# A two-layer diffusion trunk: all elementwise work of GpSimd on VectorE, and new durations in the scheduler

## The chip, the cores and the metric

The kernel runs on one core of a Trainium2 chip. The metric is the device time of one launch in microseconds, median of several runs. TensorE (PE), VectorE (DVE), ScalarE (ACT), GpSimd (POOL) and SyncE (SP) each carry out their own list of instructions in order and meet through semaphores. Here SP and POOL also issue DMAs.

## What is computed

Two layers over 256 latent and 256 context tokens with 1024 channels. A layer is a half-step SwiGLU FFN (2816 wide), a token mixer, and a second half-step FFN; each lies between a norm ahead of it (`sublayer_in`, with shift and scale from the conditioning vectors) and one behind it (`sublayer_out`, gated, onto the residual).

```python
def rmsnorm(x, g):
    xf = x.astype(jnp.float32)
    y = xf * lax.rsqrt(jnp.mean(xf * xf, axis=-1, keepdims=True) + EPS)
    return (y * g.astype(jnp.float32)).astype(x.dtype)

def sublayer_in(h, g_pre, mod, s):
    return rmsnorm(h, g_pre) * (1 + mod[:, 3 * s + 1]) + mod[:, 3 * s]

def sublayer_out(h, y, g_post, mod, s, weight):
    return h + weight * mod[:, 3 * s + 2] * rmsnorm(y, g_post)

def swiglu(h, w_gate, w_up, w_down):
    return (jax.nn.silu(h @ w_gate) * (h @ w_up)) @ w_down
...
    for l in range(DEPTH):
        last = l == DEPTH - 1
        mod_x = (silu_c @ ada_w[l] + ada_b[l]).reshape(B, N_ADA, 1, D_MODEL)
        mod_c = (silu_cc @ ada_w[l] + ada_b[l]).reshape(1, N_ADA, 1, D_MODEL)
        y = swiglu(sublayer_in(x, norm_pre[l, 0], mod_x, 0), ffn_w_gate[l, 0], ffn_w_up[l, 0], ffn_w_down[l, 0])
        x = sublayer_out(x, y, norm_post[l, 0], mod_x, 0, FFN_RESIDUAL_WEIGHT)
        ...
        y_x, y_c = token_mixer(
            sublayer_in(x, norm_pre[l, 1], mod_x, 1), sublayer_in(ctx, norm_pre[l, 1], mod_c, 1),
            cos, sin, not last, w_in[l], ...)
        x = sublayer_out(x, y_x, norm_post[l, 1], mod_x, 1, 1.0)
        y = swiglu(sublayer_in(x, norm_pre[l, 2], mod_x, 2), ffn_w_gate[l, 1], ffn_w_up[l, 1], ffn_w_down[l, 1])
        x = sublayer_out(x, y, norm_post[l, 2], mod_x, 2, FFN_RESIDUAL_WEIGHT)
        ...
    return x
```

The mixer (left out) projects its input once and runs two branches on it: latent attention with eight heads and a rotary part, and a bidirectional diagonal state-space layer (S5, 64 groups of 64 states) with a gated output. Both are projected, gated, merged and projected again. Context tokens read only context; layer 1 gives out the latent tokens alone, so its mixer's end and its second FFN work on 256 columns instead of 512.

## The kernel before

Activations stand with channels on partitions and tokens on the free axis: eight blocks of 128 channels by 512 columns, in two halves `h` = 0 and 1 of 256 columns each. Matmuls reach float32 accuracy by splitting both sides in a high and a low part: each weight block of 128x512 is loaded (`raw`), rounded by ScalarE (`whi`), and its remainder formed by VectorE (`wlo`); then three matmuls are added up (high by high, low by high, high by low). Activations are split likewise (`hhi`, `hlo` for a norm's output, `hi`, `lo` elsewhere).

The program is recorded first. `Recorder` takes every operation with the operations it depends on, `schedule` (L379) simulates the five engines with durations from `cost` (L275), latencies from `LATENCY` and prices for a switch of ScalarE's table (`TABLE`) and of TensorE's tile width (`TILE`), and picks at each moment the ready operation with the smallest key. A key is the amount of TensorE work of the main line recorded ahead of the operation; work recorded aside has a shift. What comes out is one fixed list per engine, which `emit` (L572) writes, so that every row of the trace says L576. A duration in `cost` thus never changes how long an operation takes, only the order. Building layer 1's state-space tables (`s5_build`, L1598) is a filler: during layer 0's second FFN it is shifted by `PACE_B` times the VectorE time it has used so far. Layer 0's build is paced likewise by `PACE_A`. `ada_rows` forms the conditioning rows on VectorE as another filler (`ar`, `aj`, `crow` and the accumulator `ah`).

Where one sublayer ends and the next begins, three functions work. `close` (L765) evacuates a block `y` of the output and forms for each half three tiles `tri` whose column sums are needed: the residual with itself, the output with itself, and the product of both, `xy`; TensorE sums them into the bank `misc`. `Norm.chain` (L2043) makes from these sums the inverse root of the norm behind the sublayer and, through `ve`, that of the norm ahead of the next one. Each is `rsqrt` (L719), a dozen steps on 128x64 tiles `rs` on VectorE: an integer step on the bits first, two iterations, and a 128x256 tile `sp`, which TensorE spreads over all partitions (`spread`, L755) into the banks `b1` and `b2`. `Norm.block` (L2072) then forms for each block `po` = y times b1, the new residual x + po (written over `x`, or as a new tile `xn` in layer 1's last transition, where `xonly` is set), `pn` = x times b2, and its two parts `hhi` on ScalarE and `hlo` on VectorE, with which the next matmuls begin. The transition has all this in a row for each half.

GpSimd has a share in this. In `close`, the products `xy` of 54 blocks run there; in `block`, the residual sums of 48 half-blocks and the eight `xn`. In layer 1's last transition GpSimd also multiplies the identity's columns into the first `sp` (`mask`), and the first two blocks' `po` (`EARLY` = 2), for which ScalarE copies b1 out of its bank. In the trace a product `xy` is `tri<-x,y` and a residual sum `x<-x,po` or `xn<-x,po`. GpSimd's queue also carries 322 DMA issues (staging of the state-space tables `stg`, `ur`, `ys`, `kd`, and others) and sixteen memsets `X`.

In the mixer, attention takes heads in pairs. For each, scores go into a bank, VectorE forms the maximum `mx`, ScalarE the exponential `pr` with it, and VectorE the reciprocal `ss`; `qr` is the rotary query, `qs` its share of the next scores, `rot` the rotation, `rp` the product with the sine. Between them `s5_run` (L1740) puts the S5 work of the same layer: complex products `t` with the tables `m1l`, two scans `w` over 512 columns each (TENSOR_TENSOR_SCAN), and the rotated states `X`.

## Time and profile before

| | us |
|---|---|
| runs | 2303.83, 2302.32, 2298.68 |
| median | 2302.32 |
| the profiled execution, its own time | 2301.47 |
| its span, first to last instruction | 2299.7 |
| TensorE busy | 2236.4 |
| VectorE busy | 1870.4 |
| ScalarE busy | 1034.4 |
| GpSimd busy | 297.0 |

The span is what the trace covers; 1.8 us of the profiled execution's time lie around it. Busy time counts every stretch in which at least one operation of an engine runs, and a matmul's end is modelled. "Idle before" in a row of groups is time in which the engine did nothing right before operations of that group, and the names behind `<-` are what ended it. The granted clock is TensorE's, as a share of 2.4 GHz; 0.5 is its lower level of 1.2 GHz, and a figure between is a mean over a stretch.

### The profile page before, as it was taken

What the parts mean: (1) busy time and instruction counts of PE and PEld (TensorE: products, weight loads), DVE (VectorE), ACT (ScalarE), POOL (GpSimd) and SP (SyncE); (2) the same over time, 40 slices, a digit from 0 to 9 for tenths busy, and PEclk for the clock granted to TensorE, in tenths of its full rate; (3) what the DMA queues carried; (4) which work ended last, traced back from release to release, by engine and by line L of the source; (5) the groups of instructions that cost most, each with busy time, mean ns of one, the idle gap of its engine ahead of it and who ended that gap; (6) DMA issues with size and microseconds to landing.
All of it is one profiled execution on the core that took longest, in us unless ns stands there. A gap on an engine that the chain in (4) does not pass through costs nothing.

```text
span 2299.7 us, 43776 instructions
## 1 busy us (share of the span) xinstructions
PE 2236.4 (97%) x15768; PEld 1926.3 (84%) x15768; DVE 1870.4 (81%) x4314; ACT 1034.4 (45%) x2050; POOL 297.0 (13%) x455
## 2 busy tenths in 40 slices
PE   8999999899999999999999989999999998998998
PEld 6888778787888888888888878888888897997997
DVE  4997878979989889699997999888557579886454
ACT  5332233653347644543222453333246446675452
POOL 0010011330100300200100231110003110312000
PEclk9999999999999999999999989999999999998999
DMA  9344556954975556133554644566444695773552
GB/s 312 102 163 137 172 203 205 359 199 154 319 260 172 170 163 217 48 128 117 176 183 139 210 148 158 200 213 220 152 147 150 236 319 179 186 258 111 179 193 87
DMA packets 237481, 428.06 MB, mean 186 GB/s; under 512 B 29488, under 2 KB 58032, under 8 KB 237264
## 3 DMA queue, kind: packets, MB, share of 16 engines
q1 hardware_dynamic: 213904, 350.79, 47.2%
q0 software_dynamic: 23360, 74.48, 9.2%
q8 instruction: 124, 2.03, 0.4%
q14 instruction: 93, 0.76, 0.1%
HBM read 366.56 MB, written 58.59 MB: 185 GB/s over the span
## 4 chain that ended last, share of the span: by engine, by line
PE 75%; DVE 8%; DMA 3%; issue 1%; ACT 1%; POOL 0%; DVEq 0%; SPq 0%; ACTq 0%; POOLq 0%
PE acc L576 74%; DVE rs L576 1%; DVE t L576 1%; DVE wlo L576 1%; DMA aw<-in_ada_w_dram 1%; PE misc L576 1%; DVE lo L576 1%; DVE w L576 1%; DMA ar<-in_ada_t_dram 0%; DMA m1l<-stg 0%; DMA raw<-in_w_in_dram 0%; DVE po L576 0%; DVE hlo L576 0%; DVE X L576 0%; DVE sp L576 0%
## 5 line engine op out<-in xcount | busy, mean ns | idle before, releaser
L576 PE MATMUL acc<-hhi,whi 128*128 128x256 f32 (+2 forms) x2112 | 717.8, 345 | 5.1 <-ACT hhi L576 4.2
L576 PE MATMUL acc<-hlo,whi 128*128 128x256 f32 (+2 forms) x2112 | 703.9, 344 | 4.8 <-DVE hlo L576 4.8
L576 PE MATMUL acc<-hhi,wlo 128*128 128x256 f32 (+2 forms) x2112 | 706.3, 343 | 0.5 <-DVE wlo L576 0.2
L576 ACT ACTIVATE whi<-raw 128x512 fp32r<-128x512 f32 x802 | 479.0, 624 | 366.7 <-PE acc L576 141.3
L576 DVE TENSOR_TENSOR wlo<-raw,whi 128x512 fp32r<-128x512 f32 x802 | 530.1, 689 | 133.1 <-ACT whi L576 80.3
L576 PEld LDWEIGHTS acc<-hhi,whi 128*128 128x128 f32 (+1 forms) x2112 | 398.7, 190 | 57.2 <-ACT hhi L576 7.0
L576 PEld LDWEIGHTS acc<-hhi,wlo 128*128 128x128 f32 (+1 forms) x2112 | 399.0, 190 | 49.4 <-DVE wlo L576 2.8
L576 PEld LDWEIGHTS acc<-hlo,whi 128*128 128x128 f32 (+1 forms) x2112 | 392.3, 190 | 55.2 <-DVE hlo L576 7.7
L576 PE MATMUL acc<-hi,whi 128*128 128x512 f32 (+1 forms) x1144 | 390.7, 344 | 2.4 <-DVE lo L576 2.0
L576 PE MATMUL acc<-lo,whi 128*128 128x512 f32 (+1 forms) x1144 | 388.6, 341 | 0.0
L576 PE MATMUL acc<-hi,wlo 128*128 128x512 f32 (+1 forms) x1144 | 384.2, 343 | 1.0 <-DVE wlo L576 1.0
L576 PEld LDWEIGHTS acc<-hi,whi 128*128 128x128 f32 x1144 | 215.3, 189 | 32.3 <-DVE lo L576 2.4
L576 PEld LDWEIGHTS acc<-hi,wlo 128*128 128x128 f32 x1144 | 214.4, 189 | 27.8 <-DVE wlo L576 2.2
L576 PEld LDWEIGHTS acc<-lo,whi 128*128 128x128 f32 x1144 | 215.5, 189 | 25.0 <-issue 0.9
L576 ACT ACTIVATE sg<-acc 128x512 f32<-128x512 f32 (+1 forms) x129 | 64.9, 504 | 231.5 <-PE acc L576 212.9
L576 ACT ACTIVATE hi<-sg 128x512 fp32r<-128x512 f32 (+1 forms) x113 | 60.6, 542 | 167.9 <-DVE sg L576 142.2
L576 DVE TENSOR_TENSOR sg<-sg,acc 128x512 f32<-128x512 f32 (+1 forms) x97 | 55.7, 575 | 97.0 <-ACT sg L576 62.0
L576 POOL TENSOR_TENSOR tri<-x,y 128x256 f32<-128x256 f32 x54 | 52.4, 976 | 320.5 <-ACT y L576 299.0
L576 POOL DMA_DIRECT2D stg<-P x64 | 34.8, 543 | 376.7 <-DVE P L576 360.9
L576 DVE CUSTOM_DVE_ANT_0 ar<-ar,crow,adab 128x512 f32<-128x512 f32 x104 | 79.0, 760 | 3.6 <-DMA ar<-in_ada_t_dram 3.4
L576 DVE CUSTOM_DVE_ANT_0 ar<-ar,crow,ah 128x512 f32<-128x512 f32 x104 | 79.0, 759 | 2.0 <-DMA ar<-in_ada_t_dram 1.1
L576 DVE TENSOR_TENSOR lo<-sg,hi 128x512 fp32r<-128x512 f32 (+1 forms) x113 | 65.6, 586 | 16.9 <-ACT hi L576 10.8
(249 smaller groups left out, 3234.5 us busy)
## 6 DMA issues: line engine op xcount, KB each, us to landing
raw<-in_w_gu_dram SPq DMA_DIRECT2D x352, 256.0 KB, 3.2
ar<-in_ada_t_dram SPq DMA_DIRECT2D x208, 256.0 KB, 3.5
raw<-in_w_dn_dram SPq DMA_DIRECT2D x176, 256.0 KB, 3.1
raw<-in_w_sq_dram SPq DMA_DIRECT2D x128, 256.0 KB, 4.3
raw<-in_w_in_dram SPq DMA_DIRECT2D x112, 256.0 KB, 5.2
m1l<-stg SPq DMA_DIRECT2D x96, 256.0 KB, 5.1
aw<-in_ada_w_dram SPq DMA_DIRECT2D x80, 256.0 KB, 5.8
stg<-P POOLq DMA_DIRECT2D x64, 256.0 KB, 3.4
```

What stands on the lines that cost most here:

```text
L576: getattr(getattr(self.tc.nc, engine), method)(*[real(v) for v in a], **{k: real(v) for k, v in kw.items()})
```

## The change

`xy` in `close`, the first `sp` in layer 1's last transition, its first two `po`, and all residual sums go to VectorE; ScalarE's copy of b1 goes away with them. GpSimd keeps the DMA issues and the memsets. `PACE_B` becomes 3.2 instead of 2.5. In the scheduler, a GpSimd DMA issue is taken at 545 ns instead of 1038, its data 400 ns later; a switch of TensorE's tile width at 180 instead of 90; a scan of 512 columns at 1134 ns instead of 600; a one-pass matmul of 512 columns at 226.8 instead of 215.8 and of 256 columns at 120 instead of 109; TensorE's operations with fewer than 128 columns of weights cheaper.

```diff
@@ -22,7 +22,7 @@
 FF_SEGS = (6, 6, 5, 5)
 LEAD = 6
 LATE_A, LATE_B, LATE_C, URGENT = 0, 15000, 10000, 1500
-PACE_A, PACE_B = 1.6, 2.5
+PACE_A, PACE_B = 1.6, 3.2
 WINDOW, SOON, TABLE_PULL, TILE_PULL = 15000, 0, 8000, 12000
 SLOTS, HALVES, ROWS, TRIS = 70, 8, 8, 4
 W_AHEAD = 10000
@@ -37,7 +37,7 @@
 STAT_PULL = 1000
 LAG = 0
 SLOW = 1.0
-RUSH, APART, HOLD, EARLY = False, True, 0.8, 2
+RUSH, APART, HOLD = False, True, 0.8
 FB, LAST = 22, 4
 FIRST = (5000, 1000, 1000, 1000)
 BEHIND = 1000
@@ -228,7 +228,7 @@
     LATENCY = {("PE", "PE"): 0, ("PE", "DVE"): 196, ("PE", "ACT"): 197, ("PE", "POOL"): 224, ("PE", "SP"): 190,
                ("DVE", "DVE"): 127, ("DVE", "PE"): 202, ("ACT", "ACT"): 153, ("ACT", "PE"): 230}
     SPARE = {"slot": 8}
-    TABLE, TILE = 1283, 90
+    TABLE, TILE = 1283, 180
     TABLES = {AF.Silu: 1, AF.Sigmoid: 2, AF.Exp: 3, AF.Gelu_apprx_tanh: 4}
 
     def __init__(self, tc):
@@ -277,14 +277,14 @@
         out = a[0]
         n = int(np.prod(out.shape[1:])) if isinstance(out, View) else 0
         if method == "dma_start":
-            return 1038 if eng == "POOL" else 525
+            return 545 if eng == "POOL" else 525
         if eng == "PE":
             lhs, rhs = (a[1], a[2]) if method == "matmul" else (a[1], a[2])
             passes = 1 if rhs.dt != F32 else 4 if method == "matmul" else 2
             m = max(lhs.shape[-1], 32)
-            if m < 128:
-                return 28 + max(n, m) * passes * m / 307.2
-            return 2.5 + max(n * passes / 2.4, 53.3 * min(passes, 2) * (1 if method == "transpose" else 2))
+            if m < 128 and passes > 1:
+                return 6 + n * passes * m / 307.2
+            return (13.5 if passes == 1 else 4) + n * passes / 2.4
         if eng == "ACT":
             ptr = sum(isinstance(kw.get(k), View) for k in ("bias", "scale"))
             return 155 + 0.714 * n + 60 * ptr + 70 * ("accum_out" in kw)
@@ -296,6 +296,8 @@
             return 67 + 1.04 * int(np.prod(a[1].shape[1:]))
         if method == "tensor_tensor_reduce":
             return 132 + 1.042 * n
+        if method == "tensor_tensor_scan":
+            return 67 + 2.083 * n
         if method == "reciprocal":
             return 70 + 6.2 * n
         return 67 + 1.042 * n + (62 if method == "scalar_tensor_tensor" and isinstance(a[2], View) else 0)
@@ -502,7 +504,7 @@
                 op.start = t
                 free[e] = op.end = t + op.dur + extra
                 if op.bytes:
-                    dma = max(dma, op.end + self.DMA_IN + 1000 * (e == "POOL")) + op.bytes / 360.0
+                    dma = max(dma, op.end + self.DMA_IN + 1400 * (e == "POOL")) + op.bytes / 360.0
                     op.end = dma
                 if op.main:
                     self.front = max(self.front, op.key)
@@ -716,11 +718,10 @@
             out = self.region(r, n)[32 * j:32 * j + 32].rearrange("p (r k) -> p r k", r=n)
             self.nc.tensor.matmul(out, self.ones, q[:, :, j], start=False, stop=False, skip_group_check=True)
 
-    def rsqrt(self, v, plain=False, wide=True, times=1.0, mask=None):
+    def rsqrt(self, v, plain=False, wide=True, times=1.0):
 
         nc = self.nc
         end = 1.875 * times
-        mask = mask or nc.vector
         n = v.shape[-1]
         y, w, z = (self.blk(n, name="rs") for _ in range(3))
         nc.vector.tensor_scalar(y.bitcast(I32), v.bitcast(I32), -0.5, 1595932665.0, op0=ALU.mult, op1=ALU.add)
@@ -733,7 +734,7 @@
         diagonal = self.ident[:, 0:128:32].unsqueeze(2).to_broadcast([128, 4, 64])
         for c in range(0, n if wide else 0, 64):
             r = self.blk(256, name="sp").rearrange("p (j k) -> p j k", j=4)
-            mask.tensor_tensor(r, y[:, c:c + 64].unsqueeze(1).to_broadcast([128, 4, 64]), diagonal, op=ALU.mult)
+            nc.vector.tensor_tensor(r, y[:, c:c + 64].unsqueeze(1).to_broadcast([128, 4, 64]), diagonal, op=ALU.mult)
             rows.append(r)
         nc.vector.tensor_scalar(z, w, 0.375 * times, -1.25 * times, op0=ALU.mult, op1=ALU.add)
         nc.vector.tensor_tensor(z, z, w, op=ALU.mult)
@@ -779,7 +780,7 @@
         else:
             nc.scalar.activation(y, src, AF.Copy, scale=G)
             nc.scalar.activation(q2, y, AF.Square)
-            nc.gpsimd.tensor_tensor(xy, x, y, op=ALU.mult)
+            nc.vector.tensor_tensor(xy, x, y, op=ALU.mult)
         self.rec.urgent = False
         self.rec.pull = None if i < NB - 1 else STAT_PULL
         self.stat(3 * h, t, 3)
@@ -2043,7 +2044,6 @@
     def chain(self, h):
         T, v = self.T, self.T.nc.vector
         T.rec.urgent = self.xonly or RUSH
-        mask = T.nc.gpsimd if self.xonly else None
         b1, b2 = self.banks()
         self.bc[h] = T.flat(b1), T.flat(b2)
         if self.post is not None:
@@ -2054,11 +2054,8 @@
                 st = T.blk(128, name="rs")
                 v.tensor_copy(st, T.region(3 * h + 1, 2))
                 v.memset(T.region(3 * h, 3), 0.0)
-            r, rows = T.rsqrt(w, True, times=D ** 0.5, mask=mask)
+            r, rows = T.rsqrt(w, True, times=D ** 0.5)
             T.spread(b1, rows[0])
-            if self.xonly:
-                self.b1 = T.flat(T.blk(256, name="b1"))
-                T.nc.scalar.activation(self.b1, T.flat(b1), AF.Copy)
             a = T.blk(64, name="rs")
             v.tensor_tensor(a, r, st[:, 0:64], op=ALU.mult)
             v.scalar_tensor_tensor(a, st[:, 64:128], 2.0, a, op0=ALU.mult, op1=ALU.add)
@@ -2075,14 +2072,12 @@
         xv = T.part(T.x[i][:], h)
         c = i * 2 + h
         if self.post is not None:
-            t, xo, e = T.flat(T.blk(256, name="po")), xv, nc.vector
+            t, xo = T.flat(T.blk(256, name="po")), xv
             if self.xonly:
                 T.x[i] = T.blk(256, name="xn")
                 xv = T.flat(T.x[i])
-                if i < EARLY:
-                    b1, e = self.b1, nc.gpsimd
-            e.tensor_tensor(t, T.part(self.y[i], h), b1, op=ALU.mult)
-            (nc.vector if i < 2 and not self.xonly else nc.gpsimd).tensor_tensor(xv, xo, t, op=ALU.add)
+            nc.vector.tensor_tensor(t, T.part(self.y[i], h), b1, op=ALU.mult)
+            nc.vector.tensor_tensor(xv, xo, t, op=ALU.add)
         A, B = T.coef[self.pre]
         if self.h[i] is None:
             n = 256 if self.xonly else 512
```

The order of all engines changes with this. VectorE has 113 operations more. Three places of its list follow; the numbers behind names tell tiles apart.

First, VectorE at layer 1's last transition, from the second `sp` on: `y` is the mixer's output, `acc` the bank with a spread root. Before:

```order
L576 TENSOR_TENSOR sp_25539<-rs_25528,ident_83 128x256
L576 TENSOR_TENSOR rs_25532<-rs_25532,rs_25526 128x64
L576 TENSOR_SCALAR rs_25544<-rs_25532 128x64
L576 TENSOR_TENSOR rs_25544<-rs_25544,rs_25532 128x64
L576 SCALAR_TENSOR_TENSOR sp_25539<-rs_25544,sp_25539 128x256
L576 TENSOR_TENSOR po_25550<-y_25234,acc_25519 128x256
L576 TENSOR_TENSOR po_25554<-y_25279,acc_25519 128x256
L576 TENSOR_TENSOR po_25558<-y_25346,acc_25519 128x256
L576 TENSOR_TENSOR pn_25560<-xn_25542,acc_25552 128x256
```

Now:

```order
L578 TENSOR_TENSOR sp_25515<-rs_25508,ident_83 128x256
L578 TENSOR_TENSOR rs_25510<-rs_25510,rs_25506 128x64
L578 TENSOR_SCALAR rs_25518<-rs_25510 128x64
L578 TENSOR_TENSOR rs_25518<-rs_25518,rs_25510 128x64
L578 SCALAR_TENSOR_TENSOR sp_25515<-rs_25518,sp_25515 128x256
L578 TENSOR_TENSOR po_25522<-y_25150,acc_25501 128x256
L578 TENSOR_TENSOR po_25526<-y_25188,acc_25501 128x256
L578 TENSOR_TENSOR xn_25528<-x_85,po_25522 128x256
L578 TENSOR_TENSOR xn_25530<-x_86,po_25526 128x256
L578 TENSOR_TENSOR pn_25532<-xn_25528,acc_25524 128x256
L578 TENSOR_TENSOR pn_25534<-xn_25530,acc_25524 128x256
```

The first two `po` and all `xn`, which were GpSimd's, stand between the root and the first `pn`; the steps of this root ahead of them are the same.

Second, VectorE from layer 0 to layer 1, at the end of the second root of one half. `P`, `PW` and `c<-bw,bw` belong to the build of layer 1's tables, `aj` and the ISA row behind it to the conditioning rows. Before:

```order
L576 TENSOR_TENSOR sp_16298<-rs_16251,ident_83 128x256
L576 TENSOR_TENSOR rs_16262<-rs_16262,rs_16236 128x64
L576 TENSOR_TENSOR po_16305<-y_12870,acc_16209 128x256
L576 TENSOR_SCALAR rs_16310<-rs_16262 128x64
L576 ISA aj_16313,c_76<-ar_15367,crow_118,ah_15802 128x512
L576 ISA c_76 128x1
L576 TENSOR_TENSOR rs_16310<-rs_16310,rs_16262 128x64
L576 TENSOR_TENSOR P_16324<-xr_12903,pa_15013 128x512
L576 SCALAR_TENSOR_TENSOR sp_16298<-rs_16310,sp_16298 128x256
L576 TENSOR_TENSOR hlo_16337<-pn_16242,hhi_16259 128x8x32
L576 TENSOR_TENSOR x_85<-x_85,po_16305 128x8x32
L576 TENSOR_TENSOR po_16343<-y_12918,acc_16209 128x256
```

Now:

```order
L578 TENSOR_TENSOR sp_16233<-rs_16198,ident_83 128x256
L578 TENSOR_TENSOR rs_16206<-rs_16206,rs_16189 128x64
L578 TENSOR_TENSOR x_92<-x_92,po_16201 128x8x32
L578 TENSOR_SCALAR rs_16246<-rs_16206 128x64
L578 TENSOR_TENSOR hlo_16249<-pn_16226,hhi_16235 128x8x32
L578 TENSOR_TENSOR rs_16246<-rs_16246,rs_16206 128x64
L578 TENSOR_TENSOR pn_16256<-x_92,acc_15873 128x256
L578 SCALAR_TENSOR_TENSOR sp_16233<-rs_16246,sp_16233 128x256
L578 TENSOR_TENSOR c_80<-bw_15587,bw_15593 128x4x2x16 x2
L578 TENSOR_TENSOR PW_16274<-xi_13124,pa_14987 128x512
L578 TENSOR_TENSOR hlo_16279<-pn_16272,hhi_16263 128x8x32
L578 TENSOR_TENSOR P_15768<-P_15768,PW_16274 128x512
```

The residual sums `x`, GpSimd's before but for the first two blocks, stand among the steps of the root. From the last root but one to the first gate of layer 1's FFN VectorE's list has 142 operations before, 13 of them of the build, and 133 now, 8 of the build, with eight `tri` and eight `x` among them that were GpSimd's.

Third, VectorE at the last head pair of layer 1's attention, from the scans on (a scan is printed as SCALAR_TENSOR_TENSOR `w<-t,t`). Before:

```order
L576 SCALAR_TENSOR_TENSOR w_23298<-t_23230,t_23224 128x512
L576 SCALAR_TENSOR_TENSOR w_23308<-t_23230,t_23236 128x512
L576 TENSOR_TENSOR t_23224<-w_23298,m1l_22412 128x8x32
L576 TENSOR_TENSOR t_23230<-w_23308,m1l_22423 128x8x32
L576 TENSOR_TENSOR t_23236<-w_23298,m1l_22423 128x8x32
L576 TENSOR_TENSOR t_23242<-w_23308,m1l_22412 128x8x32
L576 TENSOR_TENSOR X_23346<-t_23224,t_23230 64x4x32 x2
L576 TENSOR_TENSOR X_23353<-t_23224,t_23230 64x4x32 x2
L576 TENSOR_REDUCE mx_23358<-acc_23189 128x1
```

Now, the two scans standing right ahead of these rows but one split of a weight:

```order
L578 TENSOR_TENSOR rp_23485<-sin_107,acc_23436 128x256
L578 TENSOR_TENSOR qr_23425<-qr_23425,cos_106 128x256
L578 TENSOR_TENSOR lo_23494<-acc_23415,hi_23458 128x512
L578 TENSOR_TENSOR qr_23425<-qr_23425,rp_23485 128x256
L578 TENSOR_TENSOR lo_23504<-acc_23419,hi_23465 128x512
L578 TENSOR_TENSOR t_23352<-w_23450,m1l_22748 128x8x32
L578 TENSOR_TENSOR qs_23508<-qr_23425,qs_23508 64x256
L578 TENSOR_TENSOR qs_23511<-qr_23425,qs_23511 64x256
L578 TENSOR_TENSOR t_23360<-w_23468,m1l_22755 128x8x32
L578 TENSOR_TENSOR t_23370<-w_23450,m1l_22755 128x8x32
L578 TENSOR_TENSOR olo_23536<-acc_23472,ohi_23524 128x256
L578 TENSOR_REDUCE mx_23545<-acc_23423 128x1
```

The rotary step (`rp`, `qr`, `qs`) of the next pair and splits `lo` of other operands stand between the scans and the maximum `mx`, where before the S5 products stood alone.

## Rows read from the trace of the kernel before

**Rows 1.** The page's table of engines, over the span.

```profile
PE 2236.4 (97%) x15768; PEld 1926.3 (84%) x15768; DVE 1870.4 (81%) x4314; ACT 1034.4 (45%) x2050; POOL 297.0 (13%) x455
```

**Rows 2.** Stretches: us, busy PE, PEld, DVE, ACT, POOL, clock, DMA, GB/s.

```profile
100.00:200.00 100.00, 100.00 (x443) 82.81 (x442) 91.88 (x197) 31.19 (x52) 10.83 (x20) 1.00 0.46 151
...
1330.00:1380.00 50.00, 42.22 (x358) 36.36 (x358) 48.39 (x135) 29.87 (x64) 15.90 (x23) 0.86 0.39 134
1950.00:1962.00 12.00, 7.60 (x37) 6.17 (x36) 11.03 (x32) 4.98 (x11) 0.54 (x1) 0.86 0.64 224
2085.00:2105.00 20.00, 10.40 (x75) 8.00 (x74) 17.38 (x49) 11.15 (x24) 8.05 (x11) 0.66 0.17 55
```

**Rows 3.** TensorE's waits over the span: us in total, times, longest us.

```profile
PE acc L576 <- DVE sp L576: 8.4, 5, 4.6
...
PE acc L576 <- ACT pr L576: 4.2, 2, 4.0
```

**Rows 4.** Groups by shape, span: count, busy us, mean ns, idle before.

```profile
L576 POOL TENSOR_TENSOR tri<-x,y 128x256 f32<-128x256 f32 x54 | 52.4, 976 | 320.5 <-ACT y L576 299.0 <-PE misc L576 7.0 <-issue 6.7
L576 POOL TENSOR_TENSOR x<-x,po 128x256 f32<-128x256 f32 x48 | 40.8, 863 | 64.1 <-DVE po L576 59.5 <-ACT y L576 4.2
...
L576 DVE TENSOR_TENSOR_SCAN w<-t,t 128x512 f32<-128x512 f32 x32 | 38.0, 1214 | 0.1
...
L576 DVE TENSOR_TENSOR x<-x,po 128x256 f32<-128x256 f32 x16 | 6.7, 416 | 0.0
```

**Rows 5.** Timeline, layer 1's last transition: start, us, engine, operation, idle before.

```profile
2087.75 0.20 DVE L576 TENSOR_SCALAR rs<-rs 128x64 int32<-128x64 int32 x1
...
2088.24 0.49 DVE L576 SCALAR_TENSOR_TENSOR rs<-rs,rs 128x64 f32<-128x64 f32 x2
...
2090.21 0.42 DVE L576 SCALAR_TENSOR_TENSOR sp<-rs,sp 128x256 f32<-128x256 f32 x1
...
2091.80 0.20 DVE L576 TENSOR_SCALAR rs<-rs 128x64 int32<-128x64 int32 x1
...
2092.29 0.98 DVE L576 SCALAR_TENSOR_TENSOR rs<-rs,rs 128x64 f32<-128x64 f32 x2
...
2092.46 1.41 POOL L576 TENSOR_TENSOR po<-y,b 128x256 f32<-128x256 f32 x2 [3.00 <-ACT b L576]
...
2096.01 0.42 DVE L576 SCALAR_TENSOR_TENSOR sp<-rs,sp 128x256 f32<-128x256 f32 x1
2096.35 1.07 DVE L576 TENSOR_TENSOR po<-y,acc 128x256 f32<-128x256 f32 x3
2097.88 1.08 DVE L576 TENSOR_TENSOR pn<-xn,acc 128x256 f32<-128x256 f32 x3 [0.46 <-PE acc L576]
...
2099.05 0.58 PE L576 MATMUL acc<-hhi,whi 128*128 128x256 f32 x1 [1.28 <-ACT hhi L576]
```

**Rows 6.** Layer 0 to 1: GpSimd's groups in 1330 to 1380, then timeline rows.

```profile
L576 POOL TENSOR_TENSOR x<-x,po 128x256 f32<-128x256 f32 x8 | 6.5, 830 | 6.0 <-DVE po L576 6.0
L576 POOL TENSOR_TENSOR tri<-x,y 128x256 f32<-128x256 f32 x5 | 4.5, 898 | 7.7 <-PE misc L576 3.8 <-ACT y L576 2.1 <-issue 1.8
...
1337.02 1.08 POOL L576 TENSOR_TENSOR tri<-x,y 128x256 f32<-128x256 f32 x1 [3.81 <-PE misc L576]
...
1337.40 0.76 DVE L576 TENSOR_SCALAR rs<-rs 128x64 int32<-128x64 int32 x1
...
1373.73 1.65 PE L576 MATMUL acc<-hlo,whi 128*128 128x256 f32 x6 [2.93 <-DVE hlo L576]
```

**Rows 7.** Timeline, layer 1's last head pair: DVE, ACT and PE.

```profile
1948.99 2.33 DVE L576 TENSOR_TENSOR_SCAN w<-t,t 128x512 f32<-128x512 f32 x2
...
1953.47 0.68 DVE L576 TENSOR_REDUCE mx<-acc 128x1 f32<-128x512 f32 x1
...
1954.69 0.69 ACT L576 ACTIVATE pr<-acc,mx 128x512 f32<-128x512 f32 x1 [3.58 <-DVE mx L576]
...
1955.52 0.70 PE L576 MATMUL acc<-qr,rot 128*128 128x256 f32 x2 [4.03 <-ACT pr L576]
```

## The prediction

> **What bounds the kernel now.** I read the page's table of engines first. TensorE is busy for 97% of the span, VectorE for 81%, GpSimd for 13% [rows 1]. A kernel whose TensorE is at 97% can only win in the few places where TensorE stands still or runs at the lower clock, so a sum over removed GpSimd work is worthless by itself, and I went on to the stretches. In an undisturbed FFN stretch (100 to 200 us) TensorE is busy for 100 of 100 us with 443 matmuls of 512 columns, 0.226 us each, at full clock, while VectorE is already at 92%; no edit of this kind can shorten such a stretch [rows 2]. Three stretches look otherwise, all in rows 2. From 1330 to 1380 us, the change from layer 0 to layer 1, TensorE is busy for 42.2 of 50 us at a granted clock of 0.86, and VectorE for 48.4, so VectorE is the engine that is full. From 1950 to 1962, the last attention scores of layer 1, TensorE has 7.6 of 12 us at 0.86. From 2085 to 2105, from layer 1's mixer to the last FFN, 10.4 of 20 us at 0.66, and VectorE has 17.4. The view of waits says who ends these: VectorE's `sp` rows in five waits of 8.4 us, the longest 4.6, and ScalarE's `pr`, the longest 4.0 [rows 3]. A wait is followed by a stretch at the lower of the two clock levels (a mean of 0.66 is a mix of the two), so a microsecond of wait that goes can give back up to another half or so; I count that apart. The chain that ended last is of little use here, since it names TensorE nearly throughout.
>
> **What the moved operations cost.** GpSimd has 54 products `tri`, 48 sums `x`, and in the last transition eight `xn`, two `po` and one `sp`: 113 operations of 0.7 to 0.98 us [rows 4, 5]. VectorE does the same sum in 0.416 us [rows 4], and three of its operations in a row take 1.07 us together, so the next one starts 0.33 us later [rows 5]. All 113 add 113 x 0.33 = 37 us to VectorE's 1870. That isn't yet a cost: in the stretches at 100% TensorE, VectorE has 8 us of 100 to spare.
>
> Against it stands what GpSimd's operations do to VectorE. Two `rs` operations take 0.49 us together at 2088.24 and 0.98 at 2092.29, when GpSimd's two `po` run from 2092.46 [rows 5]; an integer step of 0.20 us at 2087.75 takes 0.76 at 1337.40, inside GpSimd's `tri` of 1337.02 to 1338.10 [rows 5, 6]. So a VectorE operation that meets one of these waits some 0.25 to 0.56 us. With a meeting at every second of the 113 and 0.56 us each, 32 us come back; with none, 0; with one at each, 63. I take the middle: the move is about free in VectorE time, and what it gives is place by place.
>
> The Trainium skill (Perfetto Trace Analysis, section Optimizing Scalar/DVE Operations) says that work may be offloaded to GpSimd when VectorE is saturated, though the two share a read port and moving between them might not help. Its first half speaks against this change where VectorE is full, and by it the time would be that of the third rival below, about 2313; by its second half the time would stay at about 2302. The rows agree with both halves, the full engine of rows 2 (48.4 of 50 us) and the lengthened step of rows 6 (0.76 us for 0.20), so by that rule alone the sign is open.
>
> **The change, place by place.** *A, layer 1's mixer to the last FFN.* Here the order of work hardly changes, except that GpSimd's eleven operations stand on VectorE. The first inverse root goes from the integer step at 2087.75 to its closing `sp` at 2090.21, 2.46 us, with its first `sp` on GpSimd; the second, the same steps beside GpSimd's `po` and `xn`, takes from 2091.80 to 2096.01, 4.21 us [rows 5]. Freed, the second gets as short as the first plus its own `sp` of 0.33, 2.79: a gain of 1.42. The first gets its `sp` too, a loss of 0.33. Behind the second `sp` the first two `po` and `xn` now stand on VectorE, 4 x 0.33 = 1.32 us, where before one wait for TensorE's spread separated `po` from `pn` (2096.35 to 2097.88, 1.53 us [rows 5]): the new operations lie inside that wait. In later blocks a block costs VectorE four operations (po, xn, pn, hlo), 1.33 us, and GpSimd's 0.7 us of latency in each goes. So -1.42 + 0.33 = **-1.1 us** here. Bounds: -2.5 (the 1.28 us wait for `hhi` at 2099.05 goes as well) to +2 (the four new operations are not hidden, 1.3, and the first FFN matmul waits for two more blocks).
>
> *B, layer 1's attention.* Before, two scans of 2.33 us together stand ahead of eight products and of `mx`, whose result ScalarE's `pr` needs; `pr` waits for 3.58 us, and TensorE for 4.03 [rows 7]. The planner took a scan of 512 for 600 ns; it is 1214 [rows 4], and the change tells it 1134. In the changed order six or more operations from other groups stand between the scans and `mx`, and the rotary step `qr`, which TensorE waited on, is ahead of `mx` instead of behind. TensorE thus has work while ScalarE waits. I take the 4.03 us as gone, and leave the lower clock (12 us x 0.14 = 1.7) out as too uncertain: **-4 us**. Bounds: -5.7 (both) and +2 (the wait stays at its place and half of it appears anew at another head pair, since the order changes at all of them).
>
> *C, layer 0 to layer 1.* VectorE is full here, and TensorE loses 50 - 42.2 = 7.8 us of busy time, and up to 50 x 0.14 = 7 of clock [rows 2]. From the last inverse root but one to the first FFN gate VectorE's list has 142 operations before and 133 now: five fewer of the state-space build (13 to 8, by its slower pace), and eight `tri` and eight `x` more, of which 13 are GpSimd's in the window [rows 6]. A build operation works on 512 columns, twice those of `x`, so about 2 x 0.33 = 0.66 us: -5 x 0.66 = -3.3. Moved operations: +16 x 0.33 = +5.3. The count falls by nine in all although sixteen came and five of the build went, so twenty others lie elsewhere now: -20 x 0.33 = -6.6, of which I take half, -3.3, since they must be done somewhere near. GpSimd's blocking, 13 operations at half of 0.56: -3.6. Sum -4.9 of VectorE time, and as VectorE ends TensorE's waits here (2.93 us for `hlo` at 1373.73 [rows 6]) most of it counts: **-4 us**. Bounds: -12 (idle and two thirds of the clock) and +5.3 (the moved operations cost, nothing else comes back).
>
> *D, everything else.* The new durations reorder the whole plan. TensorE's operations are priced dearer, a 512-column matmul at 226.8 ns instead of 215.8, against 226 in the rows [rows 2]; a change of tile width at 180 instead of 90. A plan with right numbers should have fewer surprises, but each reordering has its own new ones, and no row tells their size: the other four waits for `sp` in rows 3 are 3.8 us together. GpSimd keeps its DMA issues, and nothing of arithmetic stands in front of them any more; I cost this at nothing, as no wait of rows 3 hangs on them. I take **0**, with -4 and +5 as ends (the two longest waits of rows 3, once more or once less).
>
> Sum: -1.1 - 4 - 4 + 0 = -9.1 us. The profiled execution took 2301.5 us (span 2299.7, 1.8 around it), which lies 0.85 under the median of the runs; 2301.5 - 9.1 + 0.85 = **2293 us**.
>
> **Rivals.** *No change, about 2302 (chance 0.2).* The waits only wander: TensorE still works at 97%, A is worth 1.1, and B and C lose at new places what they give. For it: TensorE waited for `sp` at five places [rows 3], and the order around each of them is new. Against it: B and C are two places with a named cause each. That the change doesn't do what it says belongs here: GpSimd's tensor operations do all go, but nothing makes TensorE wait on them directly.
>
> *Both transitions come free, about 2281 (0.1).* C yields its bound, -12, B -5.7 and A -2.5: -20. For it: VectorE at 48.4 of 50 us, so every microsecond there counts; against it: the new operations enter exactly there.
>
> *Slower, about 2313 (0.18).* VectorE saturates at the transitions: moved operations cost 0.33 us each on the path, and the blocking doesn't come back, since GpSimd's operations met VectorE where it had slack. C then loses 5.3, A 2.0; layer 0's other two transitions hold as many moved operations as C each, 2 x 5.3, a third of it on the path, 3.5; B gives nothing: 2302.3 + 10.8 = 2313. It decides when fewer than about one in four of the moved operations meets a VectorE operation for 0.56 us (0.14 us back against 0.33). For it: 92% VectorE in plain FFN stretches [rows 2]. Against it: operations lengthened at both transitions that I looked at [rows 5, 6].
>
> **How the numbers follow.** The forecast has 0.52, the rivals 0.2, 0.1 and 0.18. Within 0.2%, about 4.6 us, a measurement of this kernel can't tell a change. The forecast's own spread: half the distance to each bound, downward 0.7, 0.85, 4 and 2 for A to D, upward 1.55, 3, 4.65 and 2.5, taken as independent (root of the squares), is 4.6 down and 6.3 up, 2288 to 2299. The range of 0.8 reaches over no change and to the two others, of which it holds the inner halves: **2279 to 2308**. Faster by over 0.2% (under 2297.7): 0.1, some 0.44 of the forecast's 0.52 and a quarter of no change, 0.59. Slower (over 2306.9): 0.18 and the upper tail of no change, 0.21. Between: 0.20.
>
> **What would show it.** GpSimd's part is down to DMA issues and some memsets, about 195 us busy (297 less 52.4, 40.8 and some 8 for the rest). A: from the second integer step to `sp` 2.8 us instead of 4.2, no VectorE operation of 64 columns above 0.3 us. B: no TensorE wait over 2 us on `pr`. C: TensorE's busy time between the last `y` and the first gate rises by some 4 us; if VectorE is full there and `hlo` waits are as long, the step on C is wrong. In 100 to 200 us everything must stay at 0.226 per matmul; if VectorE reaches 100% there and TensorE falls under 100, the rival of saturation holds. The prediction fails above all if a new wait of 4 us or more stands at a head pair or transition where before there was none.

## The result and the profile after

The changed kernel takes 2271.6 us (median of four runs, 2270.7 to 2272.9) against 2300.5 before (four runs, 2296.0 to 2303.8): a ratio of 0.9878, interval 0.9866 to 0.9890, 28.9 us less. The direction was as forecast; the gain is three times the 9 us forecast, and the time lies below the range.

The page of the changed kernel, its span and table of engines:

```profile
span 2269.9 us, 43660 instructions
...
PE 2221.9 (98%) x15768; PEld 1915.2 (84%) x15768; DVE 1875.3 (83%) x4427; ACT 1033.2 (46%) x2049; POOL 195.7 (9%) x342
```

Against [rows 1], VectorE carries out 113 operations more and is busy for 4.9 us more: what the moved operations cost, and what GpSimd no longer holds up, cancel almost exactly, as the prediction had it. GpSimd is at 195.7 us, as forecast. TensorE's busy time still falls by 14.5 us with the same 15768 matmuls, most of it because work at the lower clock takes longer and counts as busy (told below); its idle time falls by 15.3.

Stretches of the changed kernel, columns as in [rows 2]: the plain FFN, then the counterparts of the three places (each some 20 to 40 us earlier than before):

```profile
100.00:200.00 100.00, 100.00 (x462) 82.22 (x461) 93.63 (x194) 31.00 (x52) 10.84 (x20) 1.00 0.47 150
...
1310.00:1360.00 50.00, 48.19 (x457) 43.32 (x457) 49.91 (x160) 36.29 (x78) 7.00 (x13) 1.00 0.49 167
1916.00:1928.00 12.00, 9.65 (x100) 7.97 (x100) 11.46 (x31) 7.99 (x18) 0.00 (x0) 1.00 0.25 81
2057.00:2077.00 20.00, 12.47 (x93) 10.09 (x92) 18.23 (x61) 11.43 (x25) 0.00 (x0) 0.74 0.23 75
```

The plain FFN is untouched. From layer 0 to layer 1 TensorE is busy for 48.2 of 50 us instead of 42.2, at full clock instead of 0.86, and VectorE gets through 160 operations instead of 135 in the same 50 us while being even fuller (49.9). TensorE's waits, columns as in [rows 3]:

```profile
PE acc L578 <- ACT c L578: 12.5, 1, 12.5
PE acc L578 <- DVE rs L578: 3.7, 2, 3.2
PE acc L578 <- DMA aw<-in_ada_w_dram: 3.1, 1, 3.1
PE acc L578 <- DVE sp L578: 2.8, 1, 2.8
```

The 12.5 us stand at the very start, ahead of the first matmul (6.4 before). The waits for `sp` are 2.8 us in one place instead of 8.4 in five, and `pr` is no longer among the waits.

For the places I use one figure throughout: **TensorE's lost time**. For each pair of matmuls that follow each other I take the distance of their starts, less the distance that matmuls of the first one's shape keep in undisturbed stretches (0.226 us for 512 columns, 0.1195 for 256, smaller shapes likewise); the sum over a stage holds waits, the lower clock and switches of tile width alike. Stages are cut at the norms' roots (from 40 or 50 us before the first root to 50 to 90 after the last). The useful work by this count is 2157.8 us in every kernel here. Worked out from the traces, in us; the columns from "in place" on are experiments told below (`all-pace` is the changed kernel without the new pace, `hold` the plan that holds VectorE). Each column is one execution; that of `blind` was 5.5 us shorter than its kernel's median, the others lie within about 3 of theirs.

```
us lost               before  changed in place    moves   durat.     pace all-pace   shadow    blind     hold
start (to 200 us)       22.4     25.2     21.6     22.3     22.7     22.5     23.8     23.2     22.5     21.6
layer 0: FFN 1           7.9      8.2      8.7      9.1      9.1      8.2      8.4      9.2      8.6      8.1
  FFN 1 to mixer        17.1      7.4     16.1     10.3     11.2     18.5      7.5     12.1     12.1     10.9
  mixer                 10.0      8.7      9.0     14.0      8.5      9.2      8.8      8.2      9.4     14.3
  mixer to FFN 2         7.7      4.2      6.6      4.2      7.4      7.4      4.0      6.9      7.3      4.6
  FFN 2                  1.3      0.7      1.3      1.4      4.4      0.8      3.6      0.8      0.8      1.4
layer 0 to layer 1      19.7      7.2     15.9     15.8     17.2      9.9     17.9     14.5     15.7      9.7
layer 1: FFN 1           1.7      7.3      2.0      2.5     10.4      5.0      4.1      8.0      7.2      2.0
  FFN 1 to mixer         6.6      3.2      6.3      5.4     10.2      8.5      4.4      6.3      7.5      4.9
  mixer                 22.8     17.3     24.8     18.7     18.8     23.3     16.2     18.0     16.1     21.2
  mixer to last FFN     14.3     12.2     13.7     12.4     13.9     13.9     12.1     13.1     12.5     14.8
  last FFN               1.7      1.7      1.7      1.7      1.7      1.7      1.7      1.7      1.7      1.7
sum                    133.2    103.4    127.7    117.8    135.4    128.7    112.7    122.1    121.5    115.2
```

So 29.8 us went, and over a third of it, 11.0 us, from layer 0's FFN 1 to the end of its mixer, which the prediction had left at zero. How these 11.0 divide is a matter of the cut: with one 50 us behind the last root the transition gives 6.5 and the mixer 4.0. The two rows are best read as one, in every column.

### The profile page after: what moved, and what is told of

It reads as the page before. It is cut to its first block, busy times and chain, and to the rows that moved or that the text cites. A ratio compares the mean times of both kernels' runs of the same rounds, so it can differ in the third digit from the quotient of the medians.

```text
span 2269.9 us, 43660 instructions
## 1 busy us (share of the span) xinstructions
PE 2221.9 (98%) x15768; PEld 1915.2 (84%) x15768; DVE 1875.3 (83%) x4427; ACT 1033.2 (46%) x2049; POOL 195.7 (9%) x342
## 5 line engine op out<-in xcount | busy, mean ns | idle before, releaser
L578 ACT ACTIVATE sg<-acc 128x512 f32<-128x512 f32 (+1 forms) x129 | 64.7, 503 | 218.5 <-PE acc L578 195.7
L578 ACT ACTIVATE hhi<-pn,c,cA 128x256 fp32r<-128x256 f32 x88 | 52.2, 595 | 38.2 <-DVE pn L578 36.6
```

The source lines that it names most:

```text
L578: getattr(getattr(self.tc.nc, engine), method)(*[real(v) for v in a], **{k: real(v) for k, v in kw.items()})
```

## The experiments

The change has three parts: **moves** (113 operations from GpSimd to VectorE), **durations** (the scheduler's numbers) and **pace** (`PACE_B`). The theories to tell apart: *blocking* (GpSimd's operations hold VectorE up, and without them the time is gone), *plan* (the new numbers give a better order), and later *known cost* (the plan can now reckon with time that it didn't know of). The kernel before ran beside each group of experiments, and its medians were 2299.5 to 2301.0.

### Swapping engines without a new plan

The kernel before, with the engine changed only when the finished order is written out:

```diff
             engine, method, a, kw = op.call
+            if engine == "gpsimd" and method == "tensor_tensor":
+                engine = "vector"
```

> The kernel before with its plan untouched: every queue keeps its order, but the 113 tensor operations that stood in GpSimd's queue are written into VectorE's at the planned place. Theory 'blocking' (what GpSimd's operations did to VectorE is most of the 29 us): 2275 to 2285. Theory 'plan' (the new durations and thus the new order are most of it): 2295 to 2305, since what comes back from blocking, some 32 us of VectorE time, is about what the moved operations cost, 37 us.

Measured: 2295.4 us, ratio 0.9980 (0.9971 to 0.9989), 4.9 us less. In the range of the theory of the plan, at its lower end. Its page and TensorE's wait at the attention of layer 1:

```profile
PE 2236.2 (97%) x15768; PEld 1924.6 (84%) x15768; DVE 1873.9 (82%) x4427; ACT 1033.2 (45%) x2050; POOL 195.2 (9%) x342
```

```profile
1948.71 1.22 PE L578 MATMUL acc<-qr,rot 128*128 128x256 f32 x2 [4.03 <-ACT pr L578]
```

VectorE's busy time is that of the changed kernel within 1.4 us, and the wait of 4.03 us for `pr` stands exactly as in [rows 7]. The same operations on the same engines as in the changed kernel, in the old order and at the old pace, are worth 5 us, not 29.

The other way round: the changed plan, with 110 of the moved operations written into GpSimd's queue at their planned place (all but the two `po` that read PSUM, and one `sp`).

```diff
-            nc.vector.tensor_tensor(xy, x, y, op=ALU.mult)
+            op = nc.vector.tensor_tensor(xy, x, y, op=ALU.mult)
+            op.call = ("gpsimd",) + op.call[1:]
...
-            nc.vector.tensor_tensor(xv, xo, t, op=ALU.add)
+            op = nc.vector.tensor_tensor(xv, xo, t, op=ALU.add)
+            if i >= 2 or self.xonly:
+                op.call = ("gpsimd",) + op.call[1:]
```

> The changed kernel with its plan untouched, but 54 products tri, 48 residual sums x and 8 sums xn are written into GpSimd's queue at their planned place (GpSimd needs 0.8 to 1.0 us for each where the plan reckons 0.33). Theory 'blocking': 2292 to 2305, the gain is gone. Theory 'plan': 2272 to 2282, most of the gain stays.

Measured: 2288.0 us, 16.4 more than the changed kernel. Between both expectations: the new order keeps 12 of its 29 us with the old engines.

### Each part alone, and every pair

Durations alone (the new `cost`, `TILE` and GpSimd latency in the kernel before):

> The kernel before with the scheduler's new durations alone (TensorE, scan, GpSimd DMA issue and latency, tile switch); GpSimd keeps its tensor operations, the pace stays 2.5. Theory 'blocking': 2295 to 2305. Theory 'plan': 2272 to 2285.

Moves and durations, without the pace:

```diff
-PACE_A, PACE_B = 1.6, 3.2
+PACE_A, PACE_B = 1.6, 2.5
```

> The changed kernel with PACE_B back at 2.5. Layer 0 to layer 1 (some 60 us around the second inverse root) lost 19.5 us of TensorE time before and 6.8 after. If the slower pace of layer 1's build frees that place: 2277 to 2284, with the loss there back at 12 or more. If the moves or the durations do: 2269 to 2275.

Moves alone, planned on VectorE with the old numbers:

> The kernel before with the 113 operations recorded and planned on VectorE (the list scheduler places them anew), but all durations and the pace as before. Measured so far: the same operations swapped in place 2295.4, durations alone 2302.7, both with pace 2.5 2282.7. Theory 'moves and durations add up': 2280, the moves are worth 20 by themselves. Theory 'they need each other' (a plan that takes a scan at half its length and TensorE too fast can't use the freed engine): 2290 to 2300.

Pace alone:

> The kernel before with PACE_B 3.2 alone. In the changed kernel the pace is worth 11 us (2282.7 against 2271.6). Theory 'the pace frees layer 0 to layer 1 whatever else': 2288 to 2292. Theory 'it pays only when VectorE isn't held up there': 2296 to 2303.

Moves and pace, with the old durations:

> The changed kernel with the old durations: moves and pace 3.2 only. Theory 'durations count': 2283 to 2293. Theory 'durations only shuffle the plan': 2268 to 2277.

Durations and pace, without the moves:

> Durations and pace 3.2 as in the changed kernel, but the 113 operations planned and run on GpSimd as before. The changed plan with 110 of them put on GpSimd gave 2288.0. Theory 'the moves are worth what that shows': 2285 to 2290. Theory 'without the moves the other two are worth nothing': 2297 to 2304.

With the kernel before and the changed one this is every combination. Medians, and what a part adds in each pair:

| moves | durations | pace | us |
|---|---|---|---|
| | | | 2300.5 |
| | | x | 2297.7 |
| | x | | 2302.7 |
| | x | x | 2296.7 |
| x | | | 2283.2 |
| x | | x | 2276.1 |
| x | x | | 2282.7 |
| x | x | x | 2271.6 |

The moves are worth 17.3, 21.6, 20.0 and 25.1 us, whatever stands beside them. The pace is worth 2.8 and 6.0 without them, 7.1 and 11.1 with them. The durations are worth +2.2, -1.0, -0.5 and -4.5: alone nothing, in the full set a little. So theory "plan" in its first form, that the measured durations bring the gain, is gone, and my expectation for durations alone under it (2272 to 2285) missed by 18 us. Of the others, pace 2.5 in the changed kernel (2282.7) and moves with pace (2276.1) lie in the range of one theory; the moves alone (2283.2) lie 3 us above the sum and below "they need each other"; the pace alone (2297.7) fits the theory that it pays only when VectorE isn't held up; and durations with pace (2296.7) lie just below the range of "worth nothing". The pace shows where it should: with 2.5 the stage from layer 0 to layer 1 loses 17.9 us, with 3.2 it loses 7.2, of which 3.2 come back as a loss in layer 1's FFN 1 (4.1 to 7.3), where more of the build stands now (134 operations instead of 93, counted in the traces). That these cause the loss isn't shown: the durations alone, at the old pace, lose 10.4 in that FFN.

### Interference alone

The changed kernel with a shadow: GpSimd repeats 110 operations into a tile that nobody reads.

```diff
+            if id(op) in self.shadow:
+                cut = (lambda v: v[:, 0:7]) if len(a[0].shape) == 3 else (lambda v: v[:, 0:224])
+                junk = View(self.junk.root, self.junk.root.base.reshape(cut(a[0]).shape), F32)
+                self.tc.nc.gpsimd.tensor_tensor(junk.real(), cut(a[1]).real(), cut(a[2]).real(), op=kw["op"])
```

> The changed kernel as it is, plus a shadow: behind 110 of the moved operations on VectorE (54 products, 48 + 8 sums) GpSimd does the same operation once more on 224 of the 256 columns, into a tile that nobody reads. Nothing waits for a result of GpSimd, so only its interference with VectorE and the later release of the inputs is left. Putting the operations themselves on GpSimd in this plan cost 16.4 us (2288.0 against 2271.6). Theory 'blocking': 2284 to 2290. Theory 'the way through GpSimd' (its 0.9 us and two hand-overs lie in the chain, blocking is hidden): 2271 to 2276.

Measured: 2292.8 us, 21.2 more than the changed kernel, above even the theory of blocking. In the view of waits of this kernel no other engine waits for GpSimd. The page, and the same place at layer 0 to 1 in two windows of eleven microseconds (columns as in [rows 2]), the shadow's first:

```profile
PE 2228.5 (97%) x15768; PEld 1918.4 (84%) x15768; DVE 1900.9 (83%) x4427; ACT 1032.6 (45%) x2049; POOL 286.7 (13%) x452
```

```profile
1314.00:1325.00 11.00, 9.13 (x75) 8.90 (x74) 10.96 (x35) 5.30 (x13) 3.62 (x5) 1.00 0.59 192
```

and the changed kernel's:

```profile
1306.00:1317.00 11.00, 10.55 (x87) 10.18 (x91) 10.96 (x43) 5.83 (x13) 0.54 (x1) 1.00 0.59 197
```

VectorE is full in both, but does 35 operations in one and 43 in the other. The timeline shows which are held; the shadow kernel:

```profile
1318.72 0.74 POOL L583 TENSOR_TENSOR junk<-x,y 128x224 f32<-128x224 f32 x1 [2.99 <-ACT y L579]
...
1318.85 0.90 DVE L579 TENSOR_TENSOR tri<-x,y 128x256 f32<-128x256 f32 x1
...
1321.45 1.34 DVE L579 TENSOR_TENSOR tri<-x,y 128x256 f32<-128x256 f32 x1
...
1324.46 0.67 DVE L579 TENSOR_SCALAR rs<-ve 128x64 f32<-128x64 f32 x1
```

the same three in the changed kernel:

```profile
1310.40 0.42 DVE L578 TENSOR_TENSOR tri<-x,y 128x256 f32<-128x256 f32 x1
...
1312.51 0.42 DVE L578 TENSOR_TENSOR tri<-x,y 128x256 f32<-128x256 f32 x1
...
1314.61 0.19 DVE L578 TENSOR_SCALAR rs<-ve 128x64 f32<-128x64 f32 x1
```

The order of the two is the same; 0.42 us becomes 0.90 and 1.34, 0.19 becomes 0.67. Over the whole shadow kernel VectorE is busy for 25.6 us longer, and the program is 21 us longer (18.6 in the profiled execution): at these places some three quarters of the time that the plan doesn't know of go through to the end. The way through GpSimd (its 0.9 us and two hand-overs) isn't needed for a cost of this size. One thing isn't separated: the repeats also stand ahead of GpSimd's DMA issues, though the swap in place, which clears the queue of arithmetic as well, gave only 5 us.

Which operations? Products or sums alone, recorded, planned and run on GpSimd again:

> The changed kernel with the 54 products xy recorded, planned and run on GpSimd again; the sums stay on VectorE. All 113 on GpSimd with these durations and this pace gave 2296.7, that is 25 us more than changed. If the products carry it: 2285 to 2297; if the sums do: 2271 to 2278; a share by number (54 of 113): 2283.

> The changed kernel with the 48 residual sums x and eight xn recorded, planned and run on GpSimd again; the products stay on VectorE. If the sums carry the 25 us: 2288 to 2297, since a sum stands between the root and the next matmul's operand; if the products do: 2271 to 2278.

Measured: 2288.4 us with the products there, 2290.6 with the sums: 16.8 and 19.0 more than changed. Each lies where it should if its group alone carried the 25 us, which can't hold of both (together 36). So there is no single culprit, and no share by number either (2283): either half costs two thirds or more of the whole.

A right price for GpSimd in the old plan:

```diff
-            return 150 + 2.1 * n
+            return 150 + 2.9 * n
```

> The kernel before with one number changed: a GpSimd operation of 256 columns is priced at 892 ns in the plan instead of 688 (976 and 863 were measured). If the loss before was a plan that took GpSimd for too fast: 2285 to 2293. If it is the engine itself, by its way or its blocking: 2297 to 2304.

Measured: 2308.8 us, 9 more than before, outside both expectations. A truer number for the engine that isn't the limit made the plan worse; it also shows that a single number can move a plan by 9 us.

### Does the plan's knowledge make the difference?

Moves with a new plan gave 17.3 us, the same moves in place 4.9. One way to explain the difference: the blocking was time of VectorE that the plan didn't know of; moved, the operations cost VectorE about the same, but the plan has them in its sums. The changed kernel with a plan that takes 110 of the moved operations at 20 ns:

```diff
-            nc.vector.tensor_tensor(xy, x, y, op=ALU.mult)
+            nc.vector.tensor_tensor(xy, x, y, op=ALU.mult).dur = 20
```

(the sums likewise).

> The changed kernel, but the plan takes 110 of the moved operations on VectorE (54 products, 48 + 8 sums) at 20 ns instead of 334: it places them knowing where they run, and not that they cost time. Theory 'known cost' (moved operations cost VectorE as much as blocking did, and the gain beyond the swap in place is that the plan can now reckon with it): 2282 to 2290. Theory 'freed engine' (VectorE is simply less held up): 2270 to 2276.

Measured: 2295.2 us (ten executions from 2289.7 to 2299.4), 23.6 more than changed and 5 beyond what known cost allowed. The same operations on the same engines, and four fifths of the gain are gone with the plan's knowledge.

The counterpart, the kernel before with everything on GpSimd, and a plan that holds VectorE for 300 ns at each GpSimd operation:

```diff
                 free[e] = op.end = t + op.dur + extra
+                if e == "POOL" and op.name == "tensor_tensor":
+                    free["DVE"] = max(free["DVE"], t) + 300
```

> The kernel before, all operations on GpSimd, but the plan holds VectorE for 300 ns at the start of each of GpSimd's 113 tensor operations, about what the trace shows it loses (33.8 us over 113). Theory 'known cost': 2283 to 2292. Theory 'freed engine': 2297 to 2305, since the chip does the same work in the same engines.

Measured: 2283.3 us, ratio 0.9925 (0.9910 to 0.9939): as much as the moves alone (2283.2), with not one operation moved. VectorE's busy time is that of the kernel before, 1870.4:

```profile
PE 2231.6 (98%) x15768; PEld 1921.9 (84%) x15768; DVE 1870.9 (82%) x4314; ACT 1031.0 (45%) x2050; POOL 294.6 (13%) x455
```

The place of the gain fits in part: layer 0 to layer 1 loses 9.7 us instead of 19.7; layer 0's first transition loses 10.9 instead of 17.1, but 4.3 of that come back in the mixer behind it (14.3 for 10.0). A control has the same 34 us in the plan, spread over all of VectorE's operations:

```diff
-        if engine.code in ("DVE", "ACT"):
-            op.dur *= SLOW
+        if engine.code == "DVE":
+            op.dur *= 1.018
```

> A control: the kernel before, with every VectorE duration in the plan 1.8% longer (34 us over 1870, as much as 113 holds of 300 ns), so the plan knows of the same sum of time but not where it falls. Holds at their places gave 2283.3. Theory 'known cost at its place': 2295 to 2306. Theory 'any reserve on VectorE will do': 2280 to 2290.

Measured: 2295.9 us, 5 less than before. Reserve as such is worth little; the hold at its places is worth 16, more than the 9 us by which the price above moved a plan, though each is one plan.

Then the hold together with the new durations and the pace, everything still on GpSimd:

> The kernel before with all 113 operations on GpSimd, with the change's new durations and pace 3.2, and with the plan holding VectorE for 300 ns at each of them. Durations and pace without the hold gave 2296.7; the full change 2271.6. Theory 'known cost': 2270 to 2279, the move itself is not needed. Theory 'the move counts as well' (GpSimd's way of 0.9 us, and blocking at moments that the plan can't foresee): 2280 to 2290.

Measured: 2292.2 us, only 4.5 less than without the hold (2296.7), and 21 short of the changed kernel. It lies above the bounds of both theories (2270 to 2279 and 2280 to 2290), and known cost by itself fails here. Among TensorE's waits in this kernel are

```profile
PE acc L580 <- DVE sp L580: 8.4, 4, 4.5
PE acc L580 <- DVE rs L580: 4.7, 3, 3.4
...
PE misc L580 <- POOL tri L580: 2.7, 1, 2.7
```

where the changed kernel has 2.8 and 3.7 for the first two and none for GpSimd: at one place TensorE waits for GpSimd's product itself, which no hold of VectorE takes away. Lost time, counted as above for the profiled executions of this kernel and of durations and pace without the hold (cuts 45 us ahead of the first root and 50 to 60 behind the last), falls by 3.9 from layer 0 to layer 1 and by some 2 us each at layer 0's mixer to FFN 2 and in layer 1's mixer, but rises by 6.1 in layer 1's FFN 1. So a hold of one fixed length can't stand in for the move in every plan. Why it did in one combination and hardly in the other stays open; a hold that depends on which VectorE operations fall beside GpSimd's wasn't tried.

### How far apart neighbouring plans lie

The changed kernel with `PACE_B` at 3.0 and 3.4:

> The changed kernel with PACE_B 3.0 instead of 3.2. A neighbour on the same axis, to see how much of the 11 us between 2.5 (2282.7) and 3.2 (2271.6) is a trend and how much one plan's luck. Trend: 2273 to 2277. Luck: outside 2268 to 2280 or as good as 3.2.

> The changed kernel with PACE_B 3.4 instead of 3.2. Trend of a slower pace going on: 2266 to 2270. A best place near 3.2 or luck: 2272 to 2282.

Measured: 2275.8 and 2274.9 us; the executions at 3.0 range from 2271.3 to 2277.7. The expected trend beyond 3.2 isn't there. The way from 2.5 to 3.0 (2282.7 to 2275.8) is larger than what follows, and between 3.0 and 3.4 plans differ by 3 to 4 us with no direction. Differences of that size between two plans say nothing about their cause; nothing tried here beats 2271.6.

## Why the prediction was wrong

**What bounds the kernel** was read rightly: plain FFN stretches stay at 100%, and nearly all of the gain lies in transitions and mixers.

**The balance of the move** was right in size. It had 37 us of cost against some 32 of blocking; measured in place, VectorE's busy time changes by 3.5 us. From there the reasoning failed: "the move is about free in VectorE time" was taken to mean that the move as such gives nothing, so that only three places with a named wait were worth counting. Planned anew, the moves are worth 17.3 to 25.1 us in four pairs. Two amounts that cancel in busy time didn't cancel in time, and the likely reason is that one of them stands in the plan and the other doesn't: the blind plan (2295.2) shows it with the moves in place, and the hold (2283.3) with the old durations and pace. With the new ones the hold gave only 4.5 us (2292.2), so that reason isn't shown for every plan.

**A, layer 1's last transition**: -1.1 forecast, -2.1 measured (14.3 to 12.2). The second root of the changed kernel:

```profile
2063.93 0.19 DVE L578 TENSOR_SCALAR rs<-rs 128x64 int32<-128x64 int32 x1
2064.16 0.23 DVE L578 TENSOR_TENSOR rs<-rs 128x64 f32<-128x64 f32 x1
2064.42 0.48 DVE L578 SCALAR_TENSOR_TENSOR rs<-rs,rs 128x64 f32<-128x64 f32 x2
2064.94 0.23 DVE L578 TENSOR_TENSOR rs<-rs 128x64 f32<-128x64 f32 x1
2065.08 0.42 DVE L578 TENSOR_TENSOR sp<-rs,ident 128x256 f32<-128x256 f32 x1
2065.42 0.22 DVE L578 TENSOR_TENSOR rs<-rs,rs 128x64 f32<-128x64 f32 x1
...
2066.16 0.42 DVE L578 SCALAR_TENSOR_TENSOR sp<-rs,sp 128x256 f32<-128x256 f32 x1
```

It takes 2.23 us instead of 4.21 [rows 5]; 2.79 was forecast. The `sp` is dearer than nothing and cheaper than 0.33: the steps of a root depend on each other and start some 0.26 us apart, an operation that waits for none starts 0.14 us behind a step, and with `sp` between them two steps start 0.48 apart (2064.94 and 2065.42), 0.22 more. The forecast was too long since the first root, taken as undisturbed, wasn't: before, GpSimd's own `sp` held one of its steps, at 0.53 us instead of 0.23.

```profile
2088.80 0.66 POOL L576 TENSOR_TENSOR sp<-rs,ident 128x256 f32<-128x256 f32 x1 [7.42 <-DVE rs L576]
```

```profile
2089.02 0.53 DVE L576 TENSOR_TENSOR rs<-rs,rs 128x64 f32<-128x64 f32 x1
```

So the first root's loss of 0.33 didn't come: integer step to closing `sp` takes 2.36 us instead of 2.46. Behind the second root the prediction read 1.53 us as a wait in which four operations fit. Only 0.46 of it was idle; three `po` filled the rest. The four operations fit all the same, since the third `po` moved behind the first `pn` (1.46 us from the first `po` to it now): the size came out right, the reason given for it was not.

**B, layer 1's attention**: -4 forecast, -5.5 measured for layer 1's mixer; the wait for `pr` is gone, as said. The cause was put down to the order behind the scans, and the runs bear it out: in place, with the old order, the wait stays at 4.03; with the new durations alone it is gone, and the mixer loses 18.8 instead of 22.8; with the moves alone it is 1.5. So neither the moves nor the scan's new price are needed for it; either new order will do. Two shorter waits stand at the last scores now, 1.25 us for `mx` and 1.10 for `lo`.

**C, layer 0 to layer 1**: -4 forecast, -12.5 measured at the place, of which 5.6 come back in layer 1's FFN 1: -6.9. At the place the bound of -12 was nearer than the value taken. The step that failed is what a microsecond of VectorE is worth there. With the pace alone, from 30 us ahead of these roots to the first gate, VectorE's build work falls from 19.1 to 15.8 us (29 operations to 24), just the forecast 3.3; but TensorE loses 9.8 us less (19.7 to 9.9), of which 3.3 come back in the FFN behind it. The lower clock, next, explains most of the difference. The loss that comes back was not in the working at all.

**The lower clock** was counted apart: it stands in the bounds, and in no value. Between 200 and 2200 us the granted clock was 0.50 in six stretches before, each in or right behind waits of TensorE:

```profile
959.50:966.30 6.80, 5.95 (x28) 5.95 (x29) 6.76 (x27) 5.17 (x10) 1.64 (x2) 0.50 0.01 2
1335.00:1338.40 3.40, 3.40 (x30) 2.05 (x29) 3.40 (x11) 2.72 (x7) 1.21 (x2) 0.50 0.13 45
1352.10:1355.40 3.30, 3.13 (x14) 3.13 (x15) 3.30 (x13) 2.59 (x6) 1.34 (x3) 0.50 0.20 74
1372.50:1379.30 6.80, 5.57 (x44) 4.86 (x45) 6.08 (x13) 2.37 (x6) 1.99 (x3) 0.50 0.14 51
1956.20:1959.60 3.40, 3.40 (x13) 2.81 (x12) 2.72 (x9) 1.31 (x3) 0.00 (x0) 0.50 0.28 105
2089.30:2103.00 13.70, 6.33 (x22) 4.95 (x23) 12.73 (x37) 5.49 (x12) 7.54 (x11) 0.50 0.01 1
```

In the changed kernel one is left (the first line below), and with the pace alone none from layer 0 to layer 1 (the second):

```profile
2063.20:2073.30 10.10, 6.11 (x24) 4.74 (x23) 9.71 (x34) 4.88 (x10) 0.00 (x0) 0.50 0.01 2
```

```profile
1295.00:1361.00 66.00, 62.89 (x590) 55.33 (x589) 64.86 (x187) 41.01 (x92) 24.70 (x29) 1.00 0.49 158
```

Matmuls of 256 columns start 0.213 us apart in these stretches and 0.1195 at full clock, so some 44% of the work in them is lost: of 27.8 us before about 12, of 6.1 after about 3. By this estimate 9 to 10 of the 29 us are the clock that came back with the waits that went: 5 at C, 2.6 at layer 0's mixer to FFN 2, 1.5 at B. It isn't the whole story: the shadow and the blind kernel have a single such stretch too, and are slower by 21 and 24 us.

**D, everything else** is the term that failed most. It had 0 with ends of -4 and +5; the rest changed by -15.3, while A, B and C together gave 14.5 for a forecast 9.1. Layer 0's FFN 1 to mixer and the mixer gave 11.0, its mixer to FFN 2 3.5, layer 1's first transition 3.4, layer 0's FFN 2 0.6, while the start cost 2.8 more and the first FFN 0.3. The three transitions hold 72 of the 113 operations, but the moves alone don't make this term: the 27.1 us lost in layer 0's first transition and mixer are 24.3 with the moves alone, 19.7 with the durations alone and 16.3 with both, and what the durations give there they lose in layer 0's FFN 2 and layer 1's FFN 1 when they stand alone. Why the durations pay at that place was not tried. Layer 0's mixer to FFN 2 does go with the moves: 4.2 with the moves alone, 7.4 with the durations or the pace alone. The prediction named layer 0's transitions only in the rival that was slower, as a cost of 3.5. In [rows 2] no stretch from there was read, though VectorE is nearly as full in it and GpSimd fuller; before:

```profile
400.00:460.00 60.00, 54.04 (x700) 46.02 (x688) 56.28 (x131) 38.08 (x86) 23.59 (x37) 1.00 0.97 360
```

and after:

```profile
400.00:460.00 60.00, 57.72 (x704) 50.19 (x703) 48.16 (x134) 39.21 (x89) 9.67 (x18) 1.00 0.94 345
```

TensorE is busy for 3.7 us more of these 60, and VectorE for 8.1 us less with three operations more. The windows are equal in time and not quite in work.

**The rivals.** "Both transitions come free" had the size nearest to the truth (2281; its own sum from the median gives 2282) and the wrong place: B and A are close to their bounds, C isn't once the loss behind it is counted, and what it lacks is D. The slower rival rested on moved operations that cost 0.33 us on the path. In place, where the plan doesn't know of them, they are paid for by the blocking, with 5 us left over. The no-change rival, that waits only wander, holds for the durations alone (2302.7).

The first half of the rule of the Trainium skill that was weighed there (Perfetto Trace Analysis, section Optimizing Scalar/DVE Operations: to offload from a saturated VectorE) doesn't hold here: VectorE is at 99.8% of 1310 to 1360 after the change (49.91 of 50 us), and GpSimd's share costs 17 to 25 us. The second half, that moving work between the two might not help, fits the swap in place (5 us) and not the moves with a new plan.

## What to carry to other kernels

Where an order is planned from durations, look for time that the plan doesn't contain: an engine that lengthens another's operations takes time for which nothing is placed, and an operation that costs as much but stands in the plan can be the better one (here in most of the plans tried, not in all). Before a move is called neutral, count the places where it happens, all of them, and read a stretch of each, not only those with the longest single wait; and where a wait brings the lower clock behind it, put that into the value and not into the bounds alone. Try a swap in the finished order and a new plan apart from each other, and run two neighbouring plans to learn how many microseconds are chance (here 3 to 4, and 9 for one changed price).
